# Order of the products in items that serve two row groups: feature tile by feature tile, or group by group

## The chip, the cores and the metric

The kernel runs on one core of one Trainium2 chip. The metric is the device time of one execution in microseconds (us). The number to compare is the median of several executions.

## The reference

The reference is a two-layer backbone over 512 latent tokens and 256 context tokens with 1024 features. Every layer is a SwiGLU feed-forward sub-layer (FFN), a token mixer (attention in layer 0, a state-space mixer in layer 1) and another FFN. Each is wrapped in norms and modulations. What matters here are the FFNs and the input projection of the attention, which multiply the same weights with both groups of tokens:

```python
def swiglu(h, w13, w2):
    gate, up = jnp.split(h @ w13, 2, axis=-1)
    return (jax.nn.silu(gate) * up) @ w2

h_lat = ffn_sublayer(h_lat, m_lat, 0, norm_pre[l, 0], norm_post[l, 0], ffn_w13[l, 0], ffn_w2[l, 0])
h_ctx = ffn_sublayer(h_ctx, m_ctx, 0, norm_pre[l, 0], norm_post[l, 0], ffn_w13[l, 0], ffn_w2[l, 0])
```

`D_MODEL` is 1024 and the hidden width `D_FF` is 2816. Three of the four FFNs (both of layer 0, the first of layer 1) serve latent and context. The last serves the latent alone.

## The kernel before

**Layout.** Everything is kept transposed, with features on the 128 partitions and tokens along the free axis. So 1024 features are `KT` = 8 tiles, and 2816 hidden features are 22 tiles. The two groups of tokens are called `LAT` (512 columns) and `CTX` (256 columns).

**Three products for one.** Weights and activations are 32-bit floats that are split into a high and a low part (`whi`/`wlo`, `ahi`/`alo`, `gh`/`gl`). `mm3` (lines 873 to 877) issues three matmuls for each feature tile and group: high weight by high activation (L875), high by low (L876), low by high (L877). Each has its own weight load. A matmul of LAT has 512 moving columns, one of CTX has 256.

**Items.** The work is a list of items (`Seq.item`). An item of the FFN body handles one weight unit of up to 1024 columns for both groups:
- `w13(j, jj, up, grp)` computes one hidden tile of the gate (`up` 0) or of the other half (`up` 1). It has 8 feature tiles, so 8 steps.
- `w2(ms, j0, C, ci, grp, last)` adds the contribution of `C` hidden tiles to one output tile `m`. The 22 hidden tiles are cut into chunks of 6, 5, 5 and 6. An item of the first three chunks has `C` steps. The fourth chunk's items serve LAT alone.
- `inproj(u, name)` in the attention has 8 steps.

In each step the loops run over the groups inside: three matmuls of LAT, then three of CTX, then the next feature tile. I call one such group of six matmuls a step. `banks()` gives an item one PSUM tile `mm` of 1024 columns, of which LAT uses 0 to 511 and CTX 512 to 767. There are three such tiles.

**How many.** `body()` of an FFN with two groups runs `w13` for hidden tile `lead` to 21 (`LEAD`: 4, 3 and 2 for the three FFNs), the last two of them (`LATE`) for LAT alone. That is 32, 34 and 36 items with two groups. It runs 8 `w2` items for each of the first three chunks, 24 per FFN. `attn.body()` runs 6 `inproj` items. Before the body, and after it, come stretches whose order is planned by `Flow`/`Graph` (lines 243 to 246 issue their matmuls); these handle one group at a time, as do the `w13` items that `head_items` makes for a single group.

**What happens at the end of an item.** `w13_out` (called at the end of `w13`) takes the result out of PSUM: for the gate ACT writes SiLU into `tmp` (L1074). For the other half DVE multiplies (L1077), ACT makes `gh` (L928) and DVE makes `gl` (L931). It does LAT, then CTX. `w2` ends with DVE adding to `y` (L1118), or ACT copying in the first chunk (L1116).

**Ticks.** After every step but the last, `tick` advances the plan's clock by columns/800 us. It lets deferred pieces come due (the low part of a weight tile, `w_lo`, L776) and pumps background work into the queues of the engines. In the first FFN this background work is the modulation dot products on DVE (`mod_dot`, L665). In the second and third it is the preparation of the state-space matrices (`s5_task`), which also issues matmuls on TensorE (L2154, L2192). All engines execute their instructions in the order in which the program emits them.

Of the kernel before, what the change touches and what calls it, by code (L numbers as in the profile page):

```python
# [16 lines left out]
P = 128  # L17
D = 1024
KT = D // P
# [6 lines left out]
LAT, CTX = 0, 1  # L26
WIDTH = (NL, NCX)
# [41 lines left out]
class Graph:  # L69
# [4 lines left out]
    LAT = 0.15  # L74
# [337 lines left out]
class Model:  # L412
# [609 lines left out]
    def ffn(self, l, f, a, parts, tags=None, feed=None):  # L1022
# [8 lines left out]
        st = {}  # L1031
# [36 lines left out]
        def w13_out(jj, up, grp, bk):  # L1068
            for q in grp:
                g, c0, n = q  # L1070
                cs = slice(c0, c0 + n)
                if not up:
                    st["s", jj, q] = self.tmp()
                    nc.scalar.activation(st["s", jj, q][:, :n], bk[g][:, cs], AF.Silu)  # L1074
                else:
                    t = st.pop(("s", jj, q))
                    nc.vector.tensor_tensor(t[:, :n], t[:, :n], bk[g][:, cs], op=ALU.mult)  # L1077
                    self.split_act(st["gh", g][:, jj, cs], st["gl", g][:, jj, cs], t[:, :n])

        def w13(j, jj, up, grp):  # L1080
            def go(w):
                hi, lo = w
                bk = self.banks()
                for k in range(KT):
                    ks = slice(k * P, (k + 1) * P)
                    for g, c0, n in grp:
                        cs = slice(c0, c0 + n)
                        self.mm3(bk[g][:, cs], hi[:, ks], lo[:, ks], a[g]["hi"][:, k, cs], a[g]["lo"][:, k, cs],
                                 k == 0, k == KT - 1)
                    if k < KT - 1:  # L1090
                        self.tick(sum(q[2] for q in grp) / 800.0)
                w13_out(jj, up, grp, bk)
            n = sum(q[2] for q in grp)
            u = (io["w13"][l, f, j, 1 if up else 0], SLOT)
            seq.item(go, [u], 24 * n / 2400.0)

        def w2(ms, j0, C, ci, grp, last):

            n = sum(q[2] for q in grp)

            def go(*ws):
                bks = [self.banks() for _ in ms]
                for jj, i in [(jj, i) for i in range(len(ms)) for jj in range(C - 1)] + [(C - 1, i) for i in range(len(ms))]:
                    ks = slice(jj * P, (jj + 1) * P)
                    hi, lo = ws[i]
                    for g, c0, n_ in grp:
                        self.mm3(bks[i][g][:, :n_], hi[:, ks], lo[:, ks], st["gh", g][:, jj, c0:c0 + n_],
                                 st["gl", g][:, jj, c0:c0 + n_], jj == 0, jj == C - 1)
                    if (jj, i) != (C - 1, len(ms) - 1):
                        self.tick(n / 800.0)  # L1110
                for m, bk in zip(ms, bks):
                    for q in grp:
                        g, c0, n_ = q
                        y = st["y"][g][:, m, c0:c0 + n_]
                        if ci == 0:
                            nc.scalar.activation(y, bk[g][:, :n_], AF.Copy)  # L1116
                        else:
                            nc.vector.tensor_tensor(y, bk[g][:, :n_], y, op=ALU.add)  # L1118
                        if last:
                            self.sq_acc(y, n_, m, st.setdefault(("box", q), {}), SQENG(nc, l, f, q))  # L1120
            us = [(io["w2"][l, f, m, :, j0 * P:(j0 + C) * P], C * P) for m in ms]
            seq.item(go, us, 3 * C * n * len(ms) / 2400.0)
# [137 lines left out]
    def attn(self, a, parts):  # L1260
        nc, seq, io, tc = self.nc, self.seq, self.io, self.tc
        OFF = (0, NL)
        st = {"alt": 0}
# [67 lines left out]
        def inproj(u, name):  # L1331
            def go(w):
                hi, lo = w
                bk = self.banks()
                for k in range(KT):
                    ks = slice(k * P, (k + 1) * P)
                    for g in (LAT, CTX):
                        self.mm3(bk[g], hi[:, ks], lo[:, ks], a[g]["hi"][:, k], a[g]["lo"][:, k], k == 0, k == KT - 1)
                    if k < KT - 1:
                        self.tick(sum(WIDTH) / 800.0)  # L1340
                for g in (LAT, CTX):
                    evac(name, bk[g], g)
            seq.item(go, [(io["w_in"][u], SLOT)], 24 * sum(WIDTH) / 2400.0)
# [1559 lines left out]
```

## Time and profile before

| what | value |
|---|---|
| median of 3 executions | 2962.26 us (2959.83 to 2965.41) |
| profiled execution, its own time | 2966.83 us |
| its span, first to last instruction | 2965.1 us |
| what lies around the span | 1.73 us |
| mean granted TensorE clock | 0.977 |
| PE busy | 2849.9 us, 16192 matmuls |
| stretches of the three FFN bodies with two groups | 122 to 527.5, 1123.4 to 1594.5, 1711.6 to 2176.3 us |

The page of the profile lists one execution: the busy time of each engine, the span in 40 slices, and groups of instructions by source line. PE is TensorE's matmul stream, PEld its weight loads, DVE the vector engine, ACT the scalar engine, POOL GpSimd. In the timeline a row is one instruction with its start and its length. Lengths of matmuls overlap, because the array is pipelined, so what one costs is read from start to next start.

### The profile page before, as it was taken

The page shows a single profiled execution, that of the slowest core. Times are in us where ns is not written, and L with a number is a line of the kernel's source. Part 1 is how long each engine was busy: PE and PEld are TensorE (multiplying, and loading weights), DVE is VectorE, ACT ScalarE, POOL GpSimd, SP SyncE. Part 2 cuts the span into 40 slices and gives each one's busy share as a digit, 9 for nine tenths or more (in the row PEclk, how much of TensorE's full clock was granted, in tenths as well). Part 3 has the DMA queues.
Part 4 walks back from the last instruction along what each step waited for, and adds up shares of the span by engine and source line. Part 5 has one row for each costly group of instructions (what it writes and reads, how often), then busy time and mean ns, then how long its engine had stood idle before and what let it go on. Part 6 is the DMA issues. An engine that isn't in the chain of part 4 may idle for free. (4 is left out here: it accounts for less than half of the span.)

```text
span 2965.1 us, 42324 instructions
## 1 busy us (share of the span) xinstructions
PE 2849.9 (96%) x16192; PEld 2475.4 (83%) x16192; DVE 1803.5 (61%) x3277; ACT 1020.7 (34%) x1781; POOL 735.8 (25%) x1223
## 2 busy tenths in 40 slices
PE   9999999989999989999999899999998999899997
PEld 8888888877888778888888788888887887888886
DVE  5788998684688487344544853444537794643334
ACT  2322122353677552222223422222224453432222
POOL 0000000141455240244244534244245000300001
PEclk9999999998799999999999999999999999999998
DMA  6465557532000322323223333232333562332232
GB/s 251 139 220 199 204 200 254 181 101 98 1 31 15 114 94 76 104 76 101 81 90 113 98 97 98 73 98 79 102 93 106 178 213 86 100 107 92 97 106 68
DMA packets 140955, 343.60 MB, mean 116 GB/s; under 512 B 13776, under 2 KB 61392, under 8 KB 138704
## 3 DMA queue, kind: packets, MB, share of 16 engines
q1 hardware_dynamic: 140752, 340.88, 35.1%
q8 instruction: 128, 2.10, 0.3%
q14 instruction: 75, 0.61, 0.1%
HBM read 311.54 MB, written 29.29 MB: 115 GB/s over the span
## 5 line engine op out<-in xcount | busy, mean ns | idle before, releaser
L875 PE MATMUL mm<-ahi,whi 128*128 128x512 f32 (+1 forms) x2128 | 738.9, 347 | 4.1 <-ACT ahi L2476 1.8
L876 PE MATMUL mm<-alo,whi 128*128 128x512 f32 (+1 forms) x2128 | 733.6, 345 | 3.8 <-DVE alo L383 1.5
L877 PE MATMUL mm<-ahi,wlo 128*128 128x512 f32 (+1 forms) x2128 | 727.4, 342 | 4.5 <-DVE wlo L776 4.5
L776 DVE TENSOR_TENSOR wlo<-raw,whi 128x1024 fp32r<-128x1024 f32 (+2 forms) x391 | 453.8, 1163 | 377.7 <-ACT whi L766 359.1
L766 ACT ACTIVATE whi<-raw 128x1024 fp32r<-128x1024 f32 (+2 forms) x411 | 392.9, 957 | 300.7 <-PE mm L876 165.7
L875 PEld LDWEIGHTS mm<-ahi,whi 128*128 128x128 f32 x2128 | 405.9, 191 | 60.8 <-issue 5.1
L877 PEld LDWEIGHTS mm<-ahi,wlo 128*128 128x128 f32 x2128 | 404.6, 190 | 55.7 <-DVE wlo L776 5.4
L876 PEld LDWEIGHTS mm<-alo,whi 128*128 128x128 f32 x2128 | 405.8, 191 | 52.6 <-DVE alo L383 2.4
L875 PE MATMUL mm<-gh,whi 128*128 128x512 f32 x992 | 348.8, 352 | 1.2 <-ACT gh L928 1.1
L876 PE MATMUL mm<-gl,whi 128*128 128x512 f32 x992 | 347.8, 351 | 0.5 <-DVE gl L931 0.5
L877 PE MATMUL mm<-gh,wlo 128*128 128x512 f32 x992 | 345.2, 348 | 0.0
L917 POOL TENSOR_TENSOR S<-S,tmp 128x512 f32<-128x512 f32 (+1 forms) x25 | 27.3, 1095 | 1067.4 <-ACT tmp L916 1066.9
L665 DVE SCALAR_TENSOR_TENSOR mj<-mw,cb 128x1024 bf16<-128x1024 f32 x224 | 273.8, 1222 | 14.3 <-DMA mw<-in_mod_wT_dram 9.9
L928 ACT ACTIVATE gh<-tmp 128x512 fp32r<-128x512 f32 (+1 forms) x135 | 73.8, 546 | 537.8 <-DVE tmp L1077 537.8
L875 PEld LDWEIGHTS mm<-gh,whi 128*128 128x128 f32 x992 | 187.1, 189 | 30.6 <-ACT gh L928 2.3
L876 PEld LDWEIGHTS mm<-gl,whi 128*128 128x128 f32 x992 | 187.0, 189 | 25.6 <-DVE gl L931 1.4
L877 PEld LDWEIGHTS mm<-gh,wlo 128*128 128x128 f32 x992 | 186.5, 188 | 26.0
L2181 POOL TENSOR_TENSOR s5t<-s5pw,s5bb 128x256 f32<-128x256 f32 x128 | 85.1, 692 | 440.7 <-PE mm L2192 355.8
L1077 DVE TENSOR_TENSOR tmp<-tmp,mm 128x512 f32<-128x512 f32 (+1 forms) x135 | 77.6, 575 | 191.6 <-PE mm L877 191.6
L1074 ACT ACTIVATE tmp<-mm 128x512 f32<-128x512 f32 (+1 forms) x135 | 63.3, 508 | 317.0 <-PE mm L877 313.1
L279 POOL TENSOR_TENSOR S<-S,tmp 128x256 f32<-128x256 f32 (+3 forms) x116 | 133.9, 1157 | 135.8 <-ACT tmp L276 127.7
L1118 DVE TENSOR_TENSOR y<-mm,y 128x512 f32<-128x512 f32 (+1 forms) x128 | 71.1, 586 | 109.8 <-PE mm L877 109.7
(462 smaller groups left out, 4995.3 us busy)
## 6 DMA issues: line engine op xcount, KB each, us to landing
raw<-in_w_dram SPq DMA_DIRECT2D x210, 512.0 KB, 3.3
mw<-in_mod_wT_dram SPq DMA_DIRECT2D x128, 512.0 KB, 3.5
raw<-in_w_dram SPq DMA_DIRECT2D x88, 384.0 KB, 3.2
raw<-in_w_dram SPq DMA_DIRECT2D x64, 320.0 KB, 3.0
raw<-in_w_in_dram SPq DMA_DIRECT2D x23, 512.0 KB, 3.7
raw<-in_w_out_dram SPq DMA_DIRECT2D x16, 512.0 KB, 3.3
s5v<-s5v SPq DMA_DIRECT2D x64, 128.0 KB, 2.7
s5w<-s5wo SPq DMA_DIRECT2D x32, 256.0 KB, 2.6
```

The source lines that it names most:

```text
L279: add = lambda e: lambda: e.tensor_tensor(S(), S(), q["t"][:, :n], op=ALU.add)
L665: self.nc.vector.scalar_tensor_tensor(junk, w, 1.0, self.cb[v], op0=ALU.mult, op1=ALU.mult, accum_out=self.modc[l][:, v, t:t + 1])
L766: self.nc.scalar.activation(hi[:, :n], raw[:, :n], AF.Copy)
L776: (eng or self.nc.vector).tensor_tensor(lo[:, :n], raw[:, :n], hi[:, :n].bitcast(F32), op=ALU.subtract)
L875: mm(out, whi, xhi, start=first, stop=False)
L876: mm(out, whi, xlo, start=False, stop=False)
L877: mm(out, wlo, xhi, start=False, stop=last)
L928: nc.scalar.activation(hi, src, AF.Copy)
L1074: nc.scalar.activation(st["s", jj, q][:, :n], bk[g][:, cs], AF.Silu)
L1077: nc.vector.tensor_tensor(t[:, :n], t[:, :n], bk[g][:, cs], op=ALU.mult)
L1118: nc.vector.tensor_tensor(y, bk[g][:, :n_], y, op=ALU.add)
L2181: g_.tensor_tensor(o, x, y, op=ALU.mult)
```

## The change

Items that serve two groups no longer alternate by feature tile. They issue all matmuls of LAT first and then all of CTX. In `w13` the result of a group is taken out of PSUM (`w13_out`) right after that group's matmuls are issued, so LAT's instructions for it now stand in the queues of ACT and DVE ahead of what is emitted during the matmuls of CTX. In `w2` and `inproj` the results are still taken out at the end. In `w2` the item for the first output tile (`ms[0] == 0`) keeps the last hidden tile for the end: LAT without it, CTX without it, then LAT's and CTX's product of it, because that tile was computed just before. The clock of the plan ticks after every group's piece instead of after every step, with the same total. Nothing else changes: the number of matmuls, weight loads, transfers and vector instructions is the same. Items that serve one group keep their order.

```diff
             def go(w):
                 hi, lo = w
                 bk = self.banks()
-                for k in range(KT):
-                    ks = slice(k * P, (k + 1) * P)
-                    for g, c0, n in grp:
-                        cs = slice(c0, c0 + n)
+                for q in grp:
+                    g, c0, n = q
+                    cs = slice(c0, c0 + n)
+                    for k in range(KT):
+                        ks = slice(k * P, (k + 1) * P)
                         self.mm3(bk[g][:, cs], hi[:, ks], lo[:, ks], a[g]["hi"][:, k, cs], a[g]["lo"][:, k, cs],
                                  k == 0, k == KT - 1)
-                    if k < KT - 1:
-                        self.tick(sum(q[2] for q in grp) / 800.0)
-                w13_out(jj, up, grp, bk)
+                        if (k, q) != (KT - 1, grp[-1]):
+                            self.tick(n / 800.0)
+                    w13_out(jj, up, [q], bk)
...
-                for jj, i in [(jj, i) for i in range(len(ms)) for jj in range(C - 1)] + [(C - 1, i) for i in range(len(ms))]:
-                    ks = slice(jj * P, (jj + 1) * P)
-                    hi, lo = ws[i]
-                    for g, c0, n_ in grp:
-                        self.mm3(bks[i][g][:, :n_], hi[:, ks], lo[:, ks], st["gh", g][:, jj, c0:c0 + n_],
-                                 st["gl", g][:, jj, c0:c0 + n_], jj == 0, jj == C - 1)
-                    if (jj, i) != (C - 1, len(ms) - 1):
-                        self.tick(n / 800.0)
+                hi, lo = ws[0]
+
+                cuts = [(0, C - 1), (C - 1, C)] if ms[0] == 0 else [(0, C)]
+                for lo_, hi_ in cuts:
+                    for q in grp:
+                        g, c0, n_ = q
+                        for jj in range(lo_, hi_):
+                            ks = slice(jj * P, (jj + 1) * P)
+                            self.mm3(bks[0][g][:, :n_], hi[:, ks], lo[:, ks], st["gh", g][:, jj, c0:c0 + n_],
+                                     st["gl", g][:, jj, c0:c0 + n_], jj == 0, jj == C - 1)
+                            if (jj, q) != (C - 1, grp[-1]):
+                                self.tick(n_ / 800.0)
...
-                for k in range(KT):
-                    ks = slice(k * P, (k + 1) * P)
-                    for g in (LAT, CTX):
+                for g in (LAT, CTX):
+                    for k in range(KT):
+                        ks = slice(k * P, (k + 1) * P)
                         self.mm3(bk[g], hi[:, ks], lo[:, ks], a[g]["hi"][:, k], a[g]["lo"][:, k], k == 0, k == KT - 1)
-                    if k < KT - 1:
-                        self.tick(sum(WIDTH) / 800.0)
+                        if (k, g) != (KT - 1, CTX):
+                            self.tick(WIDTH[g] / 800.0)
```

## The prediction

> **What bounds the kernel now.** I read the page first: the shares of the engines and the granted clock.
>
> ```profile
> span 2965.1 us, 42324 instructions
> ...
> PE 2849.9 (96%) x16192; PEld 2475.4 (83%) x16192; DVE 1803.5 (61%) x3277; ACT 1020.7 (34%) x1781; POOL 735.8 (25%) x1223
> ...
> PEclk9999999998799999999999999999999999999998
> ```
>
> PE is busy for 96% of the span, at nearly full clock. But an average over stages doesn't say what an item with two groups waits for. So I cut out the three FFN bodies, and a stretch inside the first, with the windows view. The columns are busy us and count for PE, PEld, DVE, ACT and POOL, then granted clock, DMA share and GB/s.
>
> ```profile
> 122.00:527.50 405.50, 404.31 (x2306) 353.06 (x2306) 363.79 (x607) 85.55 (x136) 0.00 (x0) 1.00 0.62 216
> 300.00:470.00 170.00, 170.00 (x974) 148.76 (x973) 161.71 (x276) 32.29 (x48) 0.00 (x0) 1.00 0.61 210
> 1123.40:1594.50 471.10, 471.10 (x2696) 408.93 (x2696) 236.23 (x639) 109.81 (x185) 150.66 (x362) 1.00 0.28 88
> 1711.60:2176.30 464.70, 464.70 (x2691) 404.72 (x2691) 212.93 (x495) 107.22 (x180) 181.37 (x462) 1.00 0.29 91
> ```
>
> In all three PE has no idle time to speak of (1.2 us in the first, none in the others) and the clock is granted in full. So in the bodies time is the number of matmuls times the spacing of their starts, and nothing else. In the first body DVE is a second candidate: 161.7 of 170 us between 300 and 470. In the other two it is half idle. The waits view of PE for the first body names it:
>
> ```profile
> PE mm L875 <- ACT gh L928: 0.8, 1, 0.8
> PE mm L876 <- DVE gl L931: 0.2, 1, 0.2
> ```
>
> **The spacing of matmuls, alternating and not.** This is the term that the change can touch, so I measured it from starts in the timeline of PE. First an alternating item (third FFN): one step, the start of the next, and a start ten steps after that.
>
> ```profile
> 1839.36 0.40 PE L875 MATMUL mm<-ahi,whi 128*128 128x512 f32 x1
> 1839.60 0.40 PE L876 MATMUL mm<-alo,whi 128*128 128x512 f32 x1
> 1839.83 0.39 PE L877 MATMUL mm<-ahi,wlo 128*128 128x512 f32 x1
> 1840.06 0.28 PE L875 MATMUL mm<-ahi,whi 128*128 128x256 f32 x1
> 1840.18 0.28 PE L876 MATMUL mm<-alo,whi 128*128 128x256 f32 x1
> 1840.30 0.28 PE L877 MATMUL mm<-ahi,wlo 128*128 128x256 f32 x1
> 1840.41 0.40 PE L875 MATMUL mm<-ahi,whi 128*128 128x512 f32 x1
> ...
> 1850.91 0.40 PE L875 MATMUL mm<-ahi,whi 128*128 128x512 f32 x1
> ```
>
> Ten steps take 1850.91 - 1840.41 = 10.50 us, so a step takes 1050 ns, also across the end of an item, which lies in this stretch. Second, a run of 512 columns alone: the end of the third body. By the code it has 4 `w13` items for LAT (96 matmuls), 4 `w2` items of 6 tiles (72) and 72 more in the planned stretch behind, so 240; the first row is the fourth of them and the last is the first 256-column matmul after them, 237 starts later. Third, a run of 256 columns alone: the three hidden tiles of CTX ahead of the second body, 2 x 3 x 24 = 144 matmuls; the first row is the second of them, the last the first matmul of the body, 143 starts later.
>
> ```profile
> 2176.97 0.39 PE L875 MATMUL mm<-ahi,whi 128*128 128x512 f32 x1
> ...
> 2230.69 0.28 PE L245 MATMUL mm<-ahi,whi 128*128 128x256 f32 x1
> ```
>
> ```profile
> 1106.31 0.28 PE L246 MATMUL mm<-alo,whi 128*128 128x256 f32 x1
> ...
> 1123.47 0.40 PE L875 MATMUL mm<-ahi,whi 128*128 128x512 f32 x1
> ```
>
> 53.72 / 237 = 226.7 ns for 512 columns, and 17.16 / 143 = 120.0 ns for 256. Six matmuls of a step at these spacings are 3 x 226.7 + 3 x 120.0 = 1040.1 ns. Alternating costs 1050.0. So each change from one width to the other and back costs **9.9 ns**. The rows of the step show where: the first two of 512 are about 235 ns apart instead of 227.
>
> **How many such changes go.** A step has one pair of changes. Steps now: two-group `w13` items 32 + 34 + 36 = 102, with 8 steps each: 816. `w2`: chunks of 6, 5 and 5 tiles, 8 output tiles, three FFNs: 16 x 8 x 3 = 384. `inproj`: 6 x 8 = 48. Together 1248. The `w2` part is confirmed by this row of the groups by shape, where 384 is exactly the high-by-high products of CTX:
>
> ```profile
> L875 PE MATMUL mm<-gh,whi 128*128 128x256 f32 x384 | 106.7, 278 | 0.0
> ```
>
> After the change an item keeps one pair, and the nine `w2` items with `ms[0] == 0` keep two: 102 + 72 + 9 + 6 = 189. Removed: 1248 - 189 = 1059 pairs, 1059 x 9.9 ns = **10.5 us**, all of it on PE, which is the path.
>
> **What it gives back in the second and third body.** The background task puts matmuls of its own between the steps.
>
> ```profile
> L2154 PE MATMUL mm<-s5v,s5Bd 128*64 128x144 f32 x256 | 38.2, 292 | 0.0
> L2192 PE MATMUL mm<-ident,s5t 128*128 128x128 f32 x128 | 19.2, 272 | 0.0
> ```
>
> They come in groups of 8 and of 4, so 256 / 8 + 128 / 4 = 64 groups. Today each falls at the end of a step, between CTX and LAT, where the width changes anyway. With ticks after every piece, 512 / 768 = two thirds of them, 43, fall inside a run of LAT. The price of both cases can be read. Today: three steps that follow such a group,
>
> ```profile
> 1810.93 0.49 PE L875 MATMUL mm<-gh,whi 128*128 128x512 f32 x1
> ...
> 1814.16 0.40 PE L875 MATMUL mm<-gh,whi 128*128 128x512 f32 x1
> ```
>
> 3.23 us, 0.08 more than 3 x 1.05. Inside LAT alone: eleven starts after such a group at the end of the second body,
>
> ```profile
> 1594.50 0.48 PE L875 MATMUL mm<-gh,whi 128*128 128x512 f32 x1
> ...
> 1597.13 0.39 PE L877 MATMUL mm<-gh,wlo 128*128 128x512 f32 x1
> ```
>
> 2.63 us, 0.14 more than 11 x 0.2267 = 2.494. So a group costs 0.14 - 0.08 = 0.06 us more there: 43 x 0.06 = 2.6 us. It was read at one place, and ticks of background needn't spread evenly, so the bounds are 0 and 64 x 0.06 = 3.8 us. I take 2.6.
>
> **What it gives back in the first body.** The `gh`/`gl` wait shown above is one place, the end of a chunk, where `w2` wants the last hidden tile and DVE is late with it, because its queue is full of background:
>
> ```profile
> 293.89 0.28 PE L875 MATMUL mm<-gh,whi 128*128 128x256 f32 x1
> ...
> 297.55 0.40 PE L875 MATMUL mm<-gh,whi 128*128 128x512 f32 x1
> ```
>
> Between these starts lie half a step and a step, 0.36 + 1.05 = 1.41 us by their spacing, but they are 3.66 us apart: 2.25 us are lost (the idle column shows less, since the modelled length of a waiting matmul hides a part). If DVE keeps its pace, a PE that arrives earlier only waits longer. Up to 294 there are 14 two-group `w13` items and 8 `w2` items of 6 steps, 14 x 7 + 8 x 5 - 1 = 137 removed pairs, 1.4 us. Against it, LAT's eviction now stands ahead of the background that is emitted during the matmuls of CTX, so LAT's half may be ready sooner; CTX's isn't. Bounds: 1.4 lost to 2.2 won (the whole wait). I take 0.5 lost, nearer to the loss, because CTX's half has the last word.
>
> **Steps that cost nothing.** LAT's eviction is moved ahead of up to 2.56 us of work emitted during CTX (256 x 8 / 800): pieces of background, and no weight split, since `w_lo` comes due 2.5 us into an item, before LAT's eviction at 5.12. While DVE or ACT waits for LAT's last matmul, these pieces wait behind it; before, they waited behind the eviction of the item before. Nobody on PE waits for them within an item. The rows for the evictions:
>
> ```profile
> L1077 DVE TENSOR_TENSOR tmp<-tmp,mm 128x512 f32<-128x512 f32 x80 | 54.8, 686 | 191.3 <-PE mm L877 191.3
> L1074 ACT ACTIVATE tmp<-mm 128x512 f32<-128x512 f32 x80 | 47.8, 597 | 316.9 <-PE mm L877 313.1 <-POOL s5T L2219 3.8
> ```
>
> The same number of evictions of the same length stays. Both idle times are engines waiting for PE, so PE isn't late because of them. No DMA is added or moved past another on SP's queue: weight fetches are issued at the start of an item, as before. `w2` and `inproj` still evict at the end, and the cover of three `mm` tiles stays: a tile comes back two items later.
>
> **Sum.** 10.5 - 2.6 - 0.5 = 7.4 us off. Against the profiled execution, 2966.83 - 7.4 = 2959.4 us. That execution lies 4.6 us above the median of the runs, within their spread (2959.83 to 2965.41). Taken off the median: 2962.26 - 7.4 = **2954.9 us**, 0.25% faster. About 0.2%, here 5.9 us, is what a measurement of this kernel can tell from no change. With the bounds, the gain lies between 10.5 - 3.8 - 1.4 = 5.3 and 10.5 + 2.2 = 12.7 us: 2949.6 to 2957.0.
>
> **The rivals.**
>
> *CTX waits for LAT's eviction (slower).* LAT and CTX are slices of one tile `mm`. If the order of accesses is kept for the tile and not for the slice, the first matmul of CTX, now emitted behind LAT's eviction, waits until ACT or DVE has read LAT. Place: the middle of each of the 102 two-group `w13` items. Price: 51 x 0.597 + 51 x 0.686 = 65 us without the time of the signals, giving 2962.3 - 7.4 + 65 = 3020 us. It turns the sum from 7.4 / 102 = 0.07 us per item. No row of before shows a matmul writing a half of `mm` whose other half is being read. Against it speaks `gh`, one tile for all hidden tiles of a group:
>
> ```profile
> 420.12 0.63 ACT L928 ACTIVATE gh<-tmp 128x512 fp32r<-128x512 f32 x1 [8.52 <-DVE tmp L1077]
> ...
> 420.40 0.40 PE L875 MATMUL mm<-gh,whi 128*128 128x512 f32 x1
> ```
>
> PE reads one slice of it while ACT writes another, without a wait. I give it 0.05.
>
> *The first body is DVE's.* If DVE's 95% between 300 and 470 us stands for an engine that sets the pace, the first body gains nothing. Its share is 384 steps less 32 + 24 + 3 = 59, 325 x 9.9 ns = 3.2 us. Then 10.5 - 2.6 - 3.2 = 4.7 us remain: 2957.6 us, no change. For it: DVE there waits for nothing but ACT. Against it: PE isn't idle in those 170 us. Chance 0.15.
>
> *The 9.9 ns aren't the neighbour's.* If what the step loses comes from something that stays (two activations read in turn, a tile of two banks), the spacing stays and the time is 2962 us. For it: the runs of one width are other items, some at other lines. Against it: L875 to L877 show 226.7 in their own LAT items. The Trainium skill, "TensorE: Matmul & The Clock Gate", section "Back-to-back issue gap", has this rule: spacing is columns / 2.4 plus about 2.5 ns, with no word on the neighbour. By it a step would take 975 ns in either order and the change would bring nothing. The trace disagrees in size, 226.7 and 120.0 where the rule has 215.8 and 109.2, and shows a step that is dearer than its parts. Chance 0.10.
>
> **How the numbers follow.** The forecast has 0.68, the rest 0.02. The forecast's range ends at 2957.0, and the runs of before scatter by some 3 us around their median, so about a tenth of its weight may be read as no change; the DVE case and most of the third rival are no change as well. Faster by over 0.2%: 0.65. Within: 0.28. Slower: 0.07, the first rival and a remainder. The range for 8 in 10 reaches from 2949.6 over the DVE case to 2961.0, and leaves out the tile wait and half of the third rival.
>
> **What would show it.** In the changed profile, starts inside an item should be 227 ns apart for LAT and 120 for CTX, with about 235 only at the first two of LAT. A `w13` item of 24 + 24 should take 8 x 1040.1 + 9.9 = 8331 ns instead of 8400. The second and third body should each be about 2.1 us shorter (339 and 353 removed pairs less half of the 2.6 us), and the first about 2.7. PE should show no new wait between LAT's last and CTX's first matmul. The forecast is wrong if PE's waits name L1074 or L1077 (first rival), if the wait for `gl` grows and others appear between 300 and 470 us (DVE), or if a run of LAT keeps 235 ns throughout (third).

## The result

The changed kernel takes 3081.12 us (median of 6 runs, 3074.02 to 3085.04). The kernel before, run beside it, takes 2962.89 us (6 runs, 2959.83 to 2970.25). The ratio is 1.0393, with a 95% interval of 1.038 to 1.0407: **118 us slower**, where 7 us faster was forecast. The profiled execution took 3074.02 us.

The page after, the same part as before:

```profile
span 3072.2 us, 42279 instructions
...
PE 2867.5 (93%) x16192; PEld 2469.0 (80%) x16192; DVE 1803.3 (59%) x3277; ACT 1027.1 (33%) x1781; POOL 729.8 (24%) x1223
```

The count of instructions on each engine is the same, and ACT and DVE are as busy as before. PE's share fell from 96% to 93%. The windows view, cut from the first matmul of each FFN body to the last of its two-group items:

```profile
120.48:560.97 440.49, 410.31 (x2307) 353.06 (x2305) 367.22 (x611) 88.02 (x137) 0.00 (x0) 1.00 0.59 201
1146.18:1629.02 482.84, 455.16 (x2579) 387.54 (x2577) 225.62 (x607) 104.30 (x172) 145.22 (x356) 0.99 0.26 80
1771.84:2284.68 512.84, 478.32 (x2690) 409.22 (x2689) 211.73 (x497) 110.40 (x181) 179.78 (x468) 0.98 0.26 82
```

The same stretches of the kernel before:

```profile
122.05:527.50 405.45, 404.26 (x2306) 353.00 (x2305) 363.79 (x607) 85.50 (x136) 0.00 (x0) 1.00 0.62 216
1123.47:1569.05 445.58, 445.58 (x2579) 388.06 (x2577) 223.06 (x606) 102.00 (x172) 145.92 (x356) 1.00 0.28 87
1711.65:2176.28 464.63, 464.63 (x2691) 404.65 (x2690) 212.93 (x495) 107.22 (x180) 181.34 (x462) 1.00 0.29 91
```

Together that is 1436.17 against 1315.66 us, 120.5 more, so the loss lies in the bodies. The spans of the two profiled executions differ by less, 107.1 us, mostly because the stretch between the first and the second body came out 10.8 us shorter, at a granted clock of 0.97 instead of 0.94 (first row before, second after):

```profile
527.50:1123.47 595.97, 555.87 (x3142) 473.45 (x3141) 417.30 (x724) 336.88 (x697) 229.44 (x198) 0.94 0.24 77
560.97:1146.18 585.21, 544.65 (x3142) 462.86 (x3141) 414.69 (x720) 336.27 (x696) 229.13 (x198) 0.97 0.24 78
```

PE now has 28 to 35 us without work in each body, where it had 1.2, 0 and 0. In the second and third the clock is no longer granted in full. PE's waits name the cause in their first two lines, which are new but for one wait of 0.8 us for L1077 (a line gives total us, times, longest):

```profile
PE mm L875 <- DVE tmp L1077: 59.4, 52, 3.8
PE mm L875 <- ACT tmp L1074: 33.8, 49, 0.7
```

L1074 and L1077 read LAT out of PSUM in `w13`: 49 and 52 waits, about one for each of the 51 and 51 items. The timeline in the middle of a gate item, then of the item after it:

```profile
1193.93 0.39 PE L877 MATMUL mm<-ahi,wlo 128*128 128x512 f32 x1
...
1194.35 0.60 ACT L1074 ACTIVATE tmp<-mm 128x512 f32<-128x512 f32 x1 [3.39 <-PE mm L877]
...
1195.00 0.39 PE L875 MATMUL mm<-ahi,whi 128*128 128x256 f32 x1 [0.69 <-ACT tmp L1074]
...
1195.22 0.28 PE L876 MATMUL mm<-alo,whi 128*128 128x256 f32 x1
```

```profile
1203.21 0.39 PE L877 MATMUL mm<-ahi,wlo 128*128 128x512 f32 x1
...
1203.64 0.69 DVE L1077 TENSOR_TENSOR tmp<-tmp,mm 128x512 f32<-128x512 f32 x1 [0.39 <-PE mm L877]
...
1204.38 0.39 PE L875 MATMUL mm<-ahi,whi 128*128 128x256 f32 x1 [0.78 <-DVE tmp L1077]
```

LAT's last matmul starts at 1193.93. ACT starts 0.42 us later, when that matmul is through (the drain), and reads for 0.60 us. CTX's first matmul starts 0.05 us after that. From LAT's last start to CTX's first are 1.07 us, where 0.227 would do, and the restarted stream loses another 0.1 us at its first spacing (0.22 instead of 0.12). With DVE it is 1.17 us.

The wait stands in the program and not in `kernel.py`: in the trace, 101 of the first matmuls of CTX have a semaphore to wait for, a signal from one engine to another, which ACT or DVE raises. The source has no semaphore. So the runs tell how the accesses to a tile are kept in order. They don't tell whether the chip could have done both at once.

This is the first rival of the prediction, which had a chance of 0.05.

### The profile page after: what moved, and what is told of

Same layout as the page of the kernel before. It is cut to its first block, busy times and chain, and to the rows that moved or that the text cites. A ratio compares the mean times of both kernels' runs of the same rounds, so it can differ in the third digit from the quotient of the medians.

```text
span 3072.2 us, 42279 instructions
## 1 busy us (share of the span) xinstructions
PE 2867.5 (93%) x16192; PEld 2469.0 (80%) x16192; DVE 1803.3 (59%) x3277; ACT 1027.1 (33%) x1781; POOL 729.8 (24%) x1223
## 5 line engine op out<-in xcount | busy, mean ns | idle before, releaser
L875 PE MATMUL mm<-ahi,whi 128*128 128x512 f32 (+1 forms) x2128 | 753.0, 354 | 96.5 <-DVE tmp L1077 59.4
L776 DVE TENSOR_TENSOR wlo<-raw,whi 128x1024 fp32r<-128x1024 f32 (+2 forms) x391 | 451.9, 1158 | 442.8 <-ACT whi L766 425.0
L877 PEld LDWEIGHTS mm<-ahi,wlo 128*128 128x128 f32 x2128 | 411.6, 193 | 51.8 <-DVE wlo L776 5.4
L876 PEld LDWEIGHTS mm<-alo,whi 128*128 128x128 f32 x2128 | 412.4, 194 | 46.1 <-DVE alo L1015 2.5
L875 PE MATMUL mm<-gh,whi 128*128 128x512 f32 (+1 forms) x992 | 347.9, 351 | 0.0
L876 PE MATMUL mm<-gl,whi 128*128 128x512 f32 (+1 forms) x992 | 346.1, 349 | 0.0
L877 PE MATMUL mm<-gh,wlo 128*128 128x512 f32 (+1 forms) x992 | 345.3, 348 | 0.0
L1074 ACT ACTIVATE tmp<-mm 128x512 f32<-128x512 f32 (+1 forms) x135 | 68.8, 510 | 439.1 <-PE mm L877 439.1
L1077 DVE TENSOR_TENSOR tmp<-tmp,mm 128x512 f32<-128x512 f32 (+1 forms) x135 | 78.0, 578 | 223.5 <-PE mm L877 223.4
```

The source lines that it names most:

```text
L776: (eng or self.nc.vector).tensor_tensor(lo[:, :n], raw[:, :n], hi[:, :n].bitcast(F32), op=ALU.subtract)
L875: mm(out, whi, xhi, start=first, stop=False)
L876: mm(out, whi, xlo, start=False, stop=False)
L877: mm(out, wlo, xhi, start=False, stop=last)
```

## The experiments

**Theory A:** accesses to the PSUM tile `mm` keep their order for the whole tile, so CTX's matmuls wait for LAT's eviction though they write another slice. The order of the products is harmless. **Theory B:** the grouped order has no gain of its own. **Theory C:** the loss comes from the eviction's early place in the queues of ACT and DVE.

### Both groups taken out at the end (e1)

```diff
-                    w13_out(jj, up, [q], bk)
+                w13_out(jj, up, grp, bk)
```

> The grouped order of the change, but w13 takes both groups out of PSUM at the end of the item, as before. Theory A (the whole loss is CTX's first matmul waiting for LAT's eviction, since both are slices of one tile; the changes of width cost 9.9 ns a pair): no wait in the middle, 10.5 us of spacing won less some 3 given back, 2955 us, ratio 0.997 to 0.998. Theory B (the order of the products itself gains nothing, the 9.9 ns is not the neighbour's): 2963 us, ratio 1.000. Theory C (the loss comes from LAT's eviction standing early in the queues of ACT and DVE and holding up what is behind it): also 2955 us.

Measured: 2964.62 us (12 runs) against 2962.45 (29 runs), ratio 1.0002 (0.9989 to 1.0014). The loss is gone, but no gain is left that the runs can show. The bodies, though, are shorter in its profile:

```profile
121.42:525.51 404.09, 402.57 (x2306) 354.36 (x2305) 363.22 (x607) 85.49 (x135) 0.00 (x0) 1.00 0.62 216
1125.58:1570.80 445.22, 444.68 (x2578) 387.91 (x2577) 222.06 (x605) 101.42 (x171) 147.22 (x356) 1.00 0.28 87
1715.24:2177.62 462.38, 462.38 (x2690) 405.01 (x2689) 212.73 (x495) 107.48 (x180) 181.22 (x467) 1.00 0.29 91
```

1311.69 us together, 4.0 less than before, at full clock. Its span is 2.2 us longer nevertheless (2967.3 against 2965.1), so the rest of that execution was 6.2 us longer, with a granted clock of 0.972 over the span against 0.977. The runs of the kernel before scatter the same way: 2954.2 us at a clock of 0.982, 2971.8 at 0.974, about 2 us for 0.001 (one run of e1 doesn't fit: 2964.57 us at 0.927). So a gain of a few us in the bodies drowns in what the clock does elsewhere. Theory B isn't refuted by the time, but by the bodies.

### A PSUM tile for each group (e2)

```diff
-                bk = self.banks()
+                bk = {}
                 for q in grp:
                     g, c0, n = q
                     cs = slice(c0, c0 + n)
+                    bk[g] = self.bank()[:, 0:WIDTH[g]]
```

> The change as it is, with LAT's eviction right after LAT's matmuls, but LAT and CTX of a w13 item get a PSUM tile each out of the same three. Theory A: CTX no longer waits for LAT's eviction, 2955 us, at most a few us more in the first body where a tile comes back sooner while DVE is late. Theory C: the early eviction stands as early in the queues as in the change, so the time stays near 3070 to 3080 us.

Measured: 2961.88 us (12 runs), ratio 0.9992 (0.998 to 1.0005). The eviction stands where the change put it, and the waits for L1074 and L1077 are gone but for two at L1077, 1.7 us together; the list of PE's waits begins with one that is in the kernel before as well:

```profile
PE st L296 <- POOL S L279: 14.0, 3, 10.0
```

```profile
121.93:524.94 403.01, 401.78 (x2306) 354.29 (x2305) 363.89 (x609) 87.86 (x137) 0.00 (x0) 1.00 0.63 218
1123.20:1567.63 444.43, 444.35 (x2579) 387.90 (x2577) 225.03 (x607) 104.23 (x172) 146.11 (x356) 1.00 0.28 87
1710.44:2172.82 462.38, 462.38 (x2690) 404.96 (x2689) 214.65 (x497) 109.85 (x181) 184.58 (x462) 1.00 0.29 91
```

1309.82 us, 5.8 less than before. Theory C falls: the early place in the queues alone costs nothing that the runs can show. The loss comes and goes with the shared tile.

### Eviction in the middle of CTX (e9)

LAT is taken out after the fourth of CTX's eight steps, from the shared tile.

```diff
-                    w13_out(jj, up, [q], bk)
+                        if len(grp) == 2 and q is grp[1] and k == 3:
+                            w13_out(jj, up, grp[:1], bk)
+                w13_out(jj, up, grp[-1:], bk)
```

> The change, with LAT's eviction in w13 written after the fourth of CTX's eight steps. If accesses to the tile keep their order as a whole, the eviction itself waits for CTX's fourth step, and the fifth waits for the eviction: the gap of about 1 us moves from the change of width to the middle of CTX's matmuls, and the time stays near 3070. If slices are told apart by their banks and the gap in the change came from elsewhere, there is none: 2960 us.

Measured: 3072.76 us (one run). The gap moved with the eviction. LAT's last matmul, CTX's first, the end of CTX's fourth step, the eviction, CTX's fifth step:

```profile
1183.14 0.39 PE L877 MATMUL mm<-ahi,wlo 128*128 128x512 f32 x1
1183.37 0.28 PE L875 MATMUL mm<-ahi,whi 128*128 128x256 f32 x1
...
1184.68 0.28 PE L877 MATMUL mm<-ahi,wlo 128*128 128x256 f32 x1
1184.99 0.60 ACT L1074 ACTIVATE tmp<-mm 128x512 f32<-128x512 f32 x1 [6.09 <-PE mm L877]
1185.64 0.38 PE L875 MATMUL mm<-ahi,whi 128*128 128x256 f32 x1 [0.69 <-ACT tmp L1074]
```

CTX now follows LAT without a gap. But ACT, idle for 6 us, doesn't start when LAT is through at 1183.53; it starts at 1184.99, 0.03 us after the last matmul of CTX that was emitted before it. So the order holds both ways, reading behind writes and writes behind reads, for slices that don't overlap. That is theory A shown directly.

An engine that reads PSUM might instead wait for the last matmul emitted, whatever its tile. The same run speaks against it. The background's copy (L2168) reads a tile of its own. The code emits it a `yield 2.0` behind its matmuls (L2161), so after further pieces of three matmuls of the item. Still it starts at 1230.42, when its own matmuls are through at 1230.38, and doesn't wait for those pieces:

```profile
1229.19 1.19 PE L2161 MATMUL mm<-s5v,s5Bd 128*64 128x144 f32 x8
...
1230.32 0.50 PE L875 MATMUL mm<-gh,whi 128*128 128x512 f32 x1
1230.42 0.35 ACT L2168 ACTIVATE s5kf<-mm 16x224 f32<-16x224 f32 x1 [0.91 <-PE mm L2161]
```

### One kind of item at a time (e4, e7)

In e4 only gate items, whose eviction is ACT's, take LAT out early; in e7 only the others, whose eviction is DVE's.

```diff
-                    w13_out(jj, up, [q], bk)
+                    if not up:                       # e7: if up
+                        w13_out(jj, up, [q], bk)
+                if up:                               # e7: if not up
+                    w13_out(jj, up, grp, bk)
```

> The grouped order; only the gate items (ACT's eviction) take LAT out early, the other half evicts both groups at the end. Theory A: 51 items wait about 0.85 us (1.075 us from LAT's last to CTX's first matmul in the changed profile, less 0.227), 43 us, so 2963 + 43 - 7.4 = 2998 us, and PE waits for L1074 alone. Theory C with DVE's queue as the place: no loss left, 2955 us.

> The grouped order; only the items of the other half (DVE's eviction) take LAT out early, the gate items evict both groups at the end. The gate's part alone cost 44 us against the version that evicts last. If the waits add up, this one costs the rest of the change's 117, some 73 us, so 3036 us: 51 waits of 0.94 us and about 25 us more where DVE comes late to the eviction because background stands ahead in its queue.

Measured: e4 3007.32 us (4 runs), ratio 1.0146 (1.013 to 1.0162), 43 us more than before; e7 3043.24 us (4 runs), ratio 1.0277 (1.0253 to 1.0301) against 2964.57, 79 us more. In e4 PE waits for L1074, 49 times, and for L1077 only the 0.8 us that the kernel before has too; in e7 it waits for L1077 alone. Both lie over what was expected, 3007 for 2998 and 3043 for 3036. The expectation of e4 left out the 0.1 us that the restarted stream loses, 5 us for 51 items, and credited the grouping with 7.4. In e7 the late evictions cost more than in the change: start to start, 14 of 50 gaps are over 1.4 us, where the change has 10. The two parts, 1.46% and 2.77%, add up to a little more than the change's 3.93%.

### CTX first (e6)

```diff
-                for q in grp:
+                for q in grp[::-1]:
...
-                        if (k, q) != (KT - 1, grp[-1]):
+                        if (k, q) != (KT - 1, grp[0]):
```

> The change with the groups of a w13 item in the other order: CTX's 256 columns first and taken out first, then LAT. If the first matmul of the second group waits for the whole eviction of the first, the wait shrinks with the eviction: 0.597 to 0.378 us for the gate, 0.686 to 0.413 for the other half, and the drain ahead of it by 0.1. So the gap from the last matmul of the first group to the first of the second falls from 1.075 and 1.169 us to about 0.75 and 0.79, and the loss against the kernel before from 118 to about 75 us: 3038 us. If instead a fixed signal or a queue made the loss, it stays near 3080.

Measured: 3094.61 us (4 runs), ratio 1.0441 (1.0418 to 1.0463). For ACT the expectation held to the digit:

```profile
1192.47 0.28 PE L877 MATMUL mm<-ahi,wlo 128*128 128x256 f32 x1
1192.79 0.38 ACT L1074 ACTIVATE tmp<-mm 128x256 f32<-128x256 f32 x1 [0.56 <-PE mm L877]
1193.22 0.50 PE L875 MATMUL mm<-ahi,whi 128*128 128x512 f32 x1 [0.47 <-ACT tmp L1074]
```

0.75 us from the last start to the next instead of 1.07: the gap is the drain, the length of the eviction and 0.05. For the total it was wrong by 57 us. DVE comes late more often, because CTX's eviction is emitted sooner in the item, where the weight split (L776) comes due: 18 of 49 gaps at L1077 are over 1.4 us, and in all 18 DVE works on a weight split between CTX's last matmul and the eviction. In the change that is so in 1 of 10. The expectation also counted from a spacing of 0.227 us, but behind a matmul of CTX the next would start after 0.12, so each of the 102 gaps loses 0.107 us more, 11 us together. And the clock suffers: windows round the three bodies (the first begins some 20 us ahead of its body) show a granted clock of 0.98, 0.99 and 0.98, over 462, 477 and 507 us.

### A change of width at every matmul (e3)

From the kernel before, with the three products of the two groups interleaved; the edit in short:

```diff
-        mm(out, whi, xhi); mm(out, whi, xlo); mm(out, wlo, xhi)      # LAT, then CTX
+        for out, x in zip(outs, xs): mm(out, whi, x[0])              # LAT, CTX
+        for out, x in zip(outs, xs): mm(out, whi, x[1])
+        for out, x in zip(outs, xs): mm(out, wlo, x[0])
```

> The kernel before, with the width changed at every matmul: in each step of two groups high-by-high of LAT, of CTX, high-by-low of LAT, of CTX, low-by-high of LAT, of CTX. Three pairs of changes in a step instead of one. If a pair costs 9.9 ns wherever it falls: 1248 x 2 x 9.9 ns = 24.7 us more, 2988 us, a step of 1070 ns. Theory B: 2963 us, a step of 1050 ns.

Measured: 2971.10 us (10 runs), ratio 1.0019 (1.0006 to 1.0032): 6 us more by the ratio, 9 by the medians, not 25.

```profile
399.83 0.51 PE L882 MATMUL mm<-ahi,whi 128*128 128x512 f32 x2
...
401.95 0.51 PE L882 MATMUL mm<-ahi,whi 128*128 128x512 f32 x2
```

Two steps in 2.12 us, so 1060 ns a step: three pairs of changes cost 20 ns over 1040, 6.7 ns each. The whole first body goes at this pace, and most of the other two. But 155 of their 755 steps take 1040 ns, as if nothing changed, 47 of them in a row behind a group of background matmuls:

```profile
1807.88 0.51 PE L882 MATMUL mm<-gh,whi 128*128 128x512 f32 x2
...
1856.76 0.51 PE L882 MATMUL mm<-ahi,whi 128*128 128x512 f32 x2
```

These 47 steps take 48.88 us, 1040 ns each. So the price of a pair isn't a constant, and it can be nothing. The other end is in e1, the first matmuls of LAT behind a run of 24 of CTX:

```profile
406.43 0.40 PE L875 MATMUL mm<-ahi,whi 128*128 128x512 f32 x1
...
407.59 0.39 PE L877 MATMUL mm<-ahi,wlo 128*128 128x512 f32 x1
...
411.44 0.39 PE L876 MATMUL mm<-alo,whi 128*128 128x512 f32 x1
```

Five spacings take 1.16 us instead of 1.134; the 17 behind them take 3.85, 226.5 ns each, which is the spacing of a run of one width. Less the 7 ns that CTX's first spacing is short (113 instead of 120 in the trace), a pair between long runs costs about **20 ns**: twice the 9.9 of a pair in a step. So a two-group item of `w13` without background work inside takes 8340 ns in e1 and e2 (median of 64 items in each), where the prediction had 8331.

### One change of width per item (e8)

From e2: the order of the groups turns round from item to item (LAT, CTX, then CTX, LAT), so that neighbouring items meet at the same width.

```diff
+    def turn(self, grp):
...
+        self.side ^= 1
+        return list(grp) if self.side else list(grp)[::-1]
...
-                for q in grp:
+                for q in self.turn(grp):
```

> The version with a PSUM tile per group, with the order of the groups turned round from item to item (LAT, CTX, then CTX, LAT), so that the width changes once per item and not twice. In the run that evicts last, a pair of changes between long runs cost 20 ns (five matmuls of LAT run wide of 227 ns), so 95 pairs fewer are 1.9 us: 2 us below the version without the turn, about 2959 to 2960 us median, ratio 0.998. If the price is 10 ns, 1 us.

Measured: 2957.69 us (12 runs) against 2964.57 (17 runs), ratio **0.9971 (0.9957 to 0.9985)**. This beats both kernels, by 7 us against the one before. e2, in its own comparison, was 0.8 per mille below; 2 us were expected between the two, and the intervals allow that. The bodies say the same without the clock's scatter:

```profile
120.35:522.85 402.50, 401.02 (x2307) 354.38 (x2305) 363.50 (x609) 86.81 (x136) 0.00 (x0) 1.00 0.62 218
1120.78:1564.64 443.86, 443.51 (x2578) 388.12 (x2577) 224.95 (x607) 103.70 (x172) 149.22 (x356) 1.00 0.28 87
1707.79:2169.89 462.10, 462.10 (x2691) 404.56 (x2690) 218.57 (x497) 110.32 (x181) 183.70 (x468) 1.00 0.29 91
```

1308.46 us together, 7.2 less than before and 1.4 less than e2.

## Why the prediction was wrong

**What bounds the kernel:** right. PE sets the pace in the bodies, and what stops PE there is the loss.

**The step that failed** is the one called "Steps that cost nothing". It asked who waits behind LAT's eviction on ACT and DVE, and said that nobody on PE does. It didn't ask who waits for the eviction through the tile. The answer was held by the first rival, and the failure is its chance of 0.05. That came from `gh`: PE reads one slice of it while ACT writes another. `gh` lies in SBUF and `mm` in PSUM, and the runs show that the two are treated differently: for `gh` slices are told apart, for `mm` they aren't (e9), and a tile for each group removes the wait (e2). Whether it is the memory that sets them apart, or that PE reads the one and writes the other, the runs don't separate. An analogy across memories was taken for evidence.

**The rival's price** was 65 us; it is 118 and more. By starts in the trace, 99 of the 102 gaps were found as such and add up to 127.0 us, where 99 x 0.227 = 22.5 would stand: 104.5 us. The prediction counted the length of the evictions, 65. It left out the drain ahead of each (0.42 us from the start of LAT's last matmul, less the 0.227 that stand anyway), the signals, and the evictions that come late. The longest of those:

```profile
1160.36 1.22 DVE L776 TENSOR_TENSOR wlo<-raw,whi 128x1024 fp32r<-128x1024 f32 x1
...
1160.71 0.39 PE L877 MATMUL mm<-ahi,wlo 128*128 128x512 f32 x1
...
1163.76 0.20 DVE L2034 TENSOR_SCALAR s5w_s5t<-s5w_s5t 128x64 f32<-128x64 f32 x1
1163.87 0.68 DVE L1077 TENSOR_TENSOR tmp<-tmp,mm 128x512 f32<-128x512 f32 x1
...
1164.61 0.58 PE L875 MATMUL mm<-ahi,whi 128*128 128x256 f32 x1 [3.51 <-DVE tmp L1077]
```

LAT was done at 1161.1, and DVE reached its eviction at 1163.87, behind a weight split and background. In the other 9 of the 10 gaps over 1.4 us at L1077 it is background alone. Before the change such lateness cost nothing, since three tiles covered it. Beside the gaps stand 0.1 us for each restart, 10 us, and the clock: in the trace's clock records 27.3 us of the three windows go at half the clock, which costs up to 13.7 us. 104.5 + 10 + 13.7 less the 4 to 6 us that the order gives (e1, e2) is 122 to 124, against 120.5 measured in the bodies.

**The spacing:** the mechanism was right in the main, its size was off. The runs of one width are 226.7 and 120.0 ns apart in the grouped items too. But the 189 pairs that stay cost 20 ns instead of 9.9 (e1), which takes 1.9 us off the 10.5. Against the 10.1 us that the sum has for the bodies alone (without the 42 pairs of `inproj`), the bodies gave 4.0 (e1) and 5.8 us (e2). What the order gives back, put at 3.1 us, fits the rest: 10.1 - 1.9 less what was measured leaves 2.4 (e2) to 4.2 us (e1). By the same working, body by body, the second and third gave back 2.2 and 3.0 us where 2.6 was put, and the first 0.2 and 1.3 where 0.5 was. The third is 2.25 us shorter in both runs, as forecast (2.1); the second only by 1.2 (e2) and 0.4 (e1). The rival that gave the 9.9 ns to something other than the neighbour isn't borne out, since the bodies did get shorter. It isn't all wrong either: in e3 the same neighbours cost 20 ns a step in one stretch and nothing in another, so something else has a part in the price. What that is, no run shows. Not borne out either is, for this kernel, the rule from the Trainium skill, "TensorE: Matmul & The Clock Gate", section "Back-to-back issue gap", by which order makes no difference; that section gives it for an isolated matmul, and here each matmul comes with a weight load in a stream.

**The DVE rival:** not borne out. The first body is 1.4 (e1) and 2.4 us (e2) shorter, against 2.7 in the sum, not unchanged.

## What to carry to other kernels

Before two engines are to work on two halves of a PSUM tile at once, see whether they are told apart: a trace in which one engine waits at a slice that nobody else touches says no, and a tile for each half says what it costs. The source needn't show such a wait: here it stood only in the program built from it. A wait that lands on the engine that sets the pace is priced from its last useful start to its next: drain, the other engine's lateness, its instruction, the restart and the clock, not the instruction alone. A gain of a few tenths of a per cent is read from stretches at full clock, because the granted clock elsewhere moves the whole by as much.

## What the runs showed of the hardware

The price of a change from 512 to 256 columns and back isn't one number: 6.7 ns a pair or, in whole stretches, nothing when every matmul changes (e3), 9.9 at three by three (the kernel before), about 20 between runs of 24 (e1, e2), where the first five matmuls of 512 run wide of 227 ns. And waits on PE cost clock only when they are long. With ACT's waits alone (e4) there is a gap of 1.07 us in every second item, none of the three bodies has a gap over 1.70 us, and their windows show a granted clock of 1.00. In the bodies of the change the clock records show six stretches at half the clock, 27.3 us together, and each begins 2.3 to 4.3 us after the start of a gap of 2.5 us or more. Behind two more gaps of that length the clock stayed full.
